# Loading two small factors ahead of the start barrier, with one of them on 32 partitions: a low-rank addition on one core

## Chip, cores, metric

One core of one Trainium2 chip. The metric is device time in microseconds (us), as a median of several executions; before the change it is 123.38 us (three runs, 123.22 to 123.45). A profile is of a single execution; its span leaves out about 1.8 us that the device time includes (121.6 against 123.4 us).

## The reference

```python
# x: (16, 512, 768) float32, A: (768, 16), B: (16, 768), scale = 0.5
lora = np.matmul(np.matmul(x, A), B)
return (x + scale * lora).astype(np.float32)
```

x is 25.2 MB and is read once and written once. A and B are 48 KB each.

## The kernel before

The rows of x are cut into 8 groups of 128 partitions x 8 rows (3 MB, 24,576 contiguous bytes per partition). For each group: ScalarE (ACT) casts x to float16, VectorE (DVE) turns it ("xt"), TensorE (PE) multiplies by A ("y_ps"), ACT writes scaled y into block diagonals ("y_diag"), PE multiplies by B ("lora_ps"), DVE adds in place and the sync queue (SP) stores. Six x buffers are there, so six groups are loaded at once and groups 6 and 7 wait for stores 0 and 1.

```python
def sync_program():
    load(0)                       # then moved into the first block, ahead of the start barrier
    ...
    for g in range(1, X_BUFS):    # X_BUFS = 6
        load(g)
    for g in range(NG - 1):
        nc.sync.wait_ge(added, 4 * (g + 1) + 2)
        nc.sync.dma_start(out=view(out2, g), in_=xs[g % X_BUFS])...
        if g == len(freed) - 1:   # after store 1: loads 6 and 7, each when its buffer is free
            ...
# the last store comes after the block
```

The setup needs A and B. GpSimd (POOL) writes selection matrices and zeros; DVE forms "a16" from A once A has landed and POOL is done; PE spreads it; DVE copies the diagonal blocks to "a_diag". B goes through "b16" and a replicating matmul to "b_rep".

```python
def scalar_program():
    nc.scalar.dma_start(out=a32, in_=A.rearrange("(p m q) r -> p m (q r)", m=NM, q=2)).then_inc(a_in, 16)
    nc.scalar.dma_start(out=b32, in_=B).then_inc(b_in, 16)      # 16 partitions, 3,072 B each
    ...
def vector_program():
    nc.vector.wait_ge(pool_done, 4)
    nc.vector.tensor_tensor(out=a16, ...)._wait_ge(a_in, 16)
    nc.vector.tensor_copy(out=b16[0:R, :], in_=b32)._wait_ge(b_in, 16)
    ...                                                         # a_diag: four copies
    nc.vector.tensor_copy(out=b_rep, in_=b_ps)...
    turn(0, 0, G // 2); turn(0, G // 2, G // 2)
```

Of the kernel before, what the change touches and what calls it, by code (L numbers as in the profile page):

```python
# [1 line left out]

# [7 lines left out]
MM_DT = mybir.dt.float16  # L10
# [4 lines left out]
Q = 32  # L15
# [3 lines left out]
def kernel(  # L19
# [14 lines left out]
    nc = tc.nc  # L34
    fp32 = mybir.dt.float32
    u32 = mybir.dt.uint32
    P = 128
    NQ = P // Q
# [3 lines left out]
    T, D = x2.shape  # L42
    R = A.shape[1]
# [3 lines left out]
    NB = W // Q  # L47
    NM = 4
    PB, PA = Q // NM, W // NM
    assert PA <= P and NM * P <= 512  # L50
    sc = float(scale)

    const = ctx.enter_context(tc.tile_pool(name="const", bufs=1))
    psum = ctx.enter_context(tc.tile_pool(name="psum", bufs=1, space=bass.MemoryType.PSUM))


    x_0 = nc.alloc_sbuf_tensor("x_0", [P, G, D], fp32).ap()
    xs = [x_0] + [const.tile([P, G, D], fp32, name=f"x_{i}") for i in range(1, X_BUFS)]
    xh = [const.tile([P, G, D], MM_DT, name=f"xh_{i}") for i in range(2)]
    xt = const.tile([P, G, W], u32, name="xt")  # L60
    y_diag = const.tile([P, G, P], MM_DT, name="y_diag")


    a32 = const.tile([PA, NM, 2 * R], fp32, name="a32")
    mine = const.tile([PA, NB], MM_DT, name="mine")
    wrap = const.tile([PB, PA], MM_DT, name="wrap")
    step = const.tile([PB, NM, NQ, Q], MM_DT, name="step")
    sel = const.tile([PA, NM, P], MM_DT, name="sel")
    b32 = const.tile([R, D], fp32, name="b32")
    rep = const.tile([Q, NQ * Q], MM_DT, name="rep")  # L70
    a16 = const.tile([PA, NM, NB, 2 * R], MM_DT, name="a16")
    b16 = const.tile([Q, D], MM_DT, name="b16")
    a_diag = const.tile([P, 2 * NB, P], MM_DT, name="a_diag")
    b_rep = const.tile([P, D], MM_DT, name="b_rep")
    y_ps = psum.tile([P, G, Q], fp32, name="y_ps")
    lora_ps = [psum.tile([P, 2, D], fp32, name=f"lora_ps_{i}") for i in range(2)]
# [8 lines left out]
    a_in, b_in = semaphore("a_in"), semaphore("b_in")  # L85
# [17 lines left out]
    def load(g):  # L103
        nc.sync.dma_start(out=xs[g % X_BUFS], in_=view(x2, g)).then_inc(loaded[g], 16)

    def sync_program():
        symbolic, nc._always_lower_symbolic_ap = nc._always_lower_symbolic_ap, False
        load(0)
        nc._always_lower_symbolic_ap = symbolic

        now, first = nc.cur_bb.bb.instructions, nc.main_func.blocks[0].instructions
        at = next(
            k for k, i in enumerate(first)
            if i.engine == mybir.EngineType.SP and isinstance(i, mybir.InstDrain)
        )
        first.insert(at, now.pop())
        for g in range(1, X_BUFS):
            load(g)
        for g in range(NG - 1):
            nc.sync.wait_ge(added, 4 * (g + 1) + 2)  # L120
            nc.sync.dma_start(out=view(out2, g), in_=xs[g % X_BUFS]).then_inc(
                freed[g] if g < len(freed) else stored, 16
            )
            if g == len(freed) - 1:
                for n in range(X_BUFS, NG):
                    nc.sync.wait_ge(freed[n - X_BUFS], 16)
                    load(n)

        nc.sync.wait_ge(added, 4 * NG + 2)
        nc.sync.sem_clear(range(nums[0], nums[-1] + 1))  # L130

    def pool_program():
        nc.gpsimd.sem_clear(stored)

        nc.gpsimd.memset(rep, 0.0)
        nc.gpsimd.memset(wrap, 0.0)
        nc.gpsimd.memset(step, 0.0)
        nc.gpsimd.memset(mine, 1.0).then_inc(pool_done, 1)
        nc.gpsimd.affine_select(
            out=rep.rearrange("i (a k) -> i a k", a=NQ),  # L140
            in_=rep.rearrange("i (a k) -> i a k", a=NQ),
            compare_op=mybir.AluOpType.not_equal, fill=1.0, base=0,
            pattern=[[0, NQ], [-1, Q]], channel_multiplier=1,
        )._wait_ge(pool_done, 1)

        nc.gpsimd.affine_select(
            out=wrap.rearrange("j (b k) -> j b k", k=PB),
            in_=wrap.rearrange("j (b k) -> j b k", k=PB),
            compare_op=mybir.AluOpType.not_equal, fill=1.0, base=0,
            pattern=[[0, NB], [-1, PB]], channel_multiplier=1,  # L150
        )

        nc.gpsimd.affine_select(
            out=step, in_=step,
            compare_op=mybir.AluOpType.not_equal, fill=1.0, base=0,
            pattern=[[1, NM], [0, NQ], [-1, Q]], channel_multiplier=NM,
        )

        nc.gpsimd.affine_select(
            out=mine, in_=mine, compare_op=mybir.AluOpType.is_ge, fill=0.0, base=0,  # L160
            pattern=[[-PB, NB]], channel_multiplier=1,
        ).then_inc(pool_done, 1)
        nc.gpsimd.affine_select(
            out=mine, in_=mine, compare_op=mybir.AluOpType.is_ge, fill=0.0, base=PB - 1,
            pattern=[[PB, NB]], channel_multiplier=-1,
        )._wait_ge(pool_done, 2).then_inc(pool_done, 1)
        nc.gpsimd.memset(b16, 0.0)
        nc.gpsimd.memset(a_diag, 0.0)
        nc.gpsimd.memset(y_diag, 0.0).then_inc(pool_done, 1)

# [4 lines left out]
        return i  # L175

    def scalar_program():
        nc.scalar.dma_start(
            out=a32, in_=A.rearrange("(p m q) r -> p m (q r)", m=NM, q=2)
        ).then_inc(a_in, 16)  # L180
        nc.scalar.dma_start(out=b32, in_=B).then_inc(b_in, 16)

        nc.scalar.copy(out=sel.rearrange("p m k -> p (m k)"), in_=sel_ps)._wait_ge(
            setup_pe, 1
        ).then_inc(setup_act, 1)
        cast(0, 0, G // 2)._wait_ge(loaded[0], 16)
        cast(0, G // 2, G // 2)
        cast(1, 0, G)._wait_ge(loaded[1], 16)
        for g in range(NG):
            for a in range(NQ):  # L190
                q = ds(a * Q, Q)
                i = nc.scalar.mul(out=y_diag[q, :, q], in_=y_ps[q, :, :], mul=sc)  # L192
                if a == 0:
                    i._wait_ge(ready, min(g + 3, NG + 1) + g + 1)
            i.then_inc(spread, 1)
            if g + 2 < NG:
                cast(g + 2, 0, G)._wait_ge(loaded[g + 2], 16)

    a_ps = lora_ps[0][:, 0, 0 : 2 * NB * R]
    b_ps = lora_ps[1][:, 0, :]  # L200
    sel_ps = lora_ps[0].rearrange("p s d -> p (s d)")[0:PA, 512 : 512 + NM * P]

    def turn(g, s0, n):
        rows = ds(s0, n)
        i = nc.vector.transpose(  # L205
            out=xt[:, rows, :].rearrange("p s w -> p (s w)"),
            in_=xh[g % 2][:, rows, :].rearrange("p s d -> p (s d)").bitcast(u32),
        )
        i.then_inc(turned, 1)
        return i  # L210

    def vector_program():
        nc.vector.wait_ge(pool_done, 4)
        nc.vector.tensor_tensor(  # L214
            out=a16,
            in0=a32[:, :, None, :].to_broadcast([PA, NM, NB, 2 * R]),
            in1=mine[:, None, :, None].to_broadcast([PA, NM, NB, 2 * R]),
            op=mybir.AluOpType.mult,
        )._wait_ge(a_in, 16).then_inc(setup_dve, 1)
        nc.vector.tensor_copy(  # L220
            out=b16[0:R, :], in_=b32
        )._wait_ge(b_in, 16).then_inc(setup_dve, 1)
        for a in range(NQ):
            q = ds(a * Q, Q)
            i = nc.vector.tensor_copy(  # L225
                out=a_diag[q, :, ds(a * Q, R)], in_=a_ps[q, :].rearrange("p (b r) -> p b r", r=R)
            )
            if a == 0:
                i._wait_ge(setup_pe, 2)
        nc.vector.tensor_copy(out=b_rep, in_=b_ps)._wait_ge(setup_pe, 3).then_inc(added, 2)  # L230
        turn(0, 0, G // 2)._wait_ge(ready, 1)
        turn(0, G // 2, G // 2)._wait_ge(ready, 2)
        for g in range(NG):
            if g + 1 < NG:
                turn(g + 1, 0, G)._wait_ge(ready, 2 * g + 4)
            for s in range(0, G, 2):
                n = (g * G + s) // 2
                rows = xs[g % X_BUFS][:, ds(s, 2), :]
                nc.vector.tensor_tensor(  # L239
                    out=rows, in0=rows, in1=lora_ps[n % 2], op=mybir.AluOpType.add  # L240
                )._wait_ge(ups, n + 1).then_inc(added, 1)

    def chunks(c0, n):

        while n:
            k = min(n, 512 - c0 % 512)
            yield c0, k
            c0, n = c0 + k, n - k

    def tensor_program():  # L250
# [9 lines left out]
            if m == 0:  # L260
                i._wait_ge(setup_dve, 1)
        i.then_inc(setup_pe, 1)
        for c0, n in chunks(0, D):
            i = nc.tensor.matmul(
                b_ps[:, ds(c0, n)], rep, b16[:, ds(c0, n)], start=True, stop=True
            )
            if c0 == 0:
                i._wait_ge(setup_dve, 2)
        i.then_inc(setup_pe, 1)
        xt_mm = xt.rearrange("p s w -> p (s w)").bitcast(MM_DT)  # L270
# [69 lines left out]
```

## Time and profile before

| what | value | view |
|---|---|---|
| device time | 123.38 us | runs |
| DMA share from 12 to 110 us | 1.00 to 1.01 | table by stretches |
| A issued, landed | 0.96, 11.4 us | timeline, chain |
| first y matmul | 21.37 us | timeline |
| last store issued | 109.83 us | timeline |
| its time to landing | 10.6 us | waits of the SP queue |
| last data packet ends | 120.4 us | packet records of the trace |

The page's DMA strip (40 equal slices, busy share of the 16 DMA engines in tenths) and its queue lines (packets, MB, share of 16 engines' span):

```profile
DMA  7999999999999999999999999999999999999990
...
q1 hardware_dynamic: 2304, 50.33, 97.3%
q10 hardware_dynamic: 144, 0.10, 0.3%
```

q1 is x in and out, q10 is A and B. The table by stretches gives start:end, length, busy time of PE, PEld, DVE, ACT and POOL with counts, the granted PE clock, the DMA share and GB/s:

```profile
0.00:3.00 3.00, 0.00 (x0) 0.00 (x0) 0.00 (x0) 0.80 (x1) 2.05 (x11) 1.00 0.79 229
...
12.00:45.00 33.00, 17.03 (x82) 9.17 (x82) 24.85 (x17) 22.52 (x13) 0.00 (x0) 0.95 1.00 429
45.00:80.00 35.00, 20.87 (x148) 13.42 (x148) 33.95 (x19) 21.21 (x18) 0.00 (x0) 1.00 1.01 431
80.00:110.00 30.00, 14.70 (x96) 8.53 (x96) 26.28 (x14) 9.33 (x12) 0.00 (x0) 0.97 1.00 432
```

No stretch between 12 and 110 us leaves the DMA engines idle, while DVE, the busiest compute engine, is nearly full in only one of them. The timeline (start us, duration us, engine, line, operation, idle time before and its releaser):

```profile
0.96 0.41 ACTq L178 DMA_DIRECT2D a_70<-in_A_dram  x1
...
11.44 1.75 DVE L214 TENSOR_TENSOR a_77<-a_70,mine 96x1536 f16<-96x1536 f32 x1 [11.44 <-DMA a_70<-in_A_dram]
...
21.37 5.20 PE L275 MATMUL y_ps<-xt,a_diag 128*128 128x256 f16 x24 [5.92 <-DVE xt L205]
...
109.83 0.33 SPq L304 DMA_DIRECT2D out_dram<-x_61  x1
```

The waits of the SP queue (who waited, for what: us in total, times, longest) end with the last store:

```profile
SPq L335 <- DMA out_dram<-x_61: 10.6, 1, 10.6
```

And the chain of work that ended last, in order of time (start, us, what), shows the first three y groups of PE:

```profile
21.37 5.21 PE y_ps L275 x24
...
34.81 3.58 PE y_ps L275 x24
...
45.98 2.69 PE y_ps L275 x24
```

After A's landing, with which it begins, this chain is made of compute throughout, because it is followed back from the last instruction that is counted; the store that follows is not in it. The chain has some 98 us of compute work almost without a gap, from 11.4 to 109.3 us.

### The profile page before, as it was taken

How to read it: one execution, taken by the hardware profiler on the slowest of the kernel's cores; microseconds unless marked ns; L12 is line 12 of the kernel's file. 1: busy time of each engine (PE TensorE's matmuls, PEld its weight loads, DVE VectorE, ACT ScalarE, POOL GpSimd, SP SyncE). 2: the span in 40 equal slices, each digit the busy share in tenths (PEclk: the TensorE clock that was granted, in tenths of full speed). 3: DMA queues.
4: the chain of work that ended last, by engine and by line, in shares of the span. 5: the costliest groups of instructions: out<-in, count | busy, mean ns of one | idle time of the engine just before them, and what ended most of it. 6: DMA issues, size and time to landing. Idle time of an engine off the chain costs nothing.

```text
span 121.6 us, 908 instructions
## 1 busy us (share of the span) xinstructions
PE 53.3 (44%) x327; PEld 31.3 (26%) x327; DVE 85.6 (70%) x48; ACT 56.5 (46%) x43; POOL 6.8 (6%) x16
## 2 busy tenths in 40 slices
PE   0200600974296449437446742943754594310000
PEld 0000100642154227216213521821432262100000
DVE  0002699029994999999999999999999982990000
ACT  2305929729903990992596299089440004000000
POOL 6950000000000000000000000000000000000000
PEclk9999999999959999999999999999999999985555
DMA  7999999999999999999999999999999999999990
GB/s 234 407 405 409 437 445 404 445 445 404 445 445 404 445 429 421 396 485 412 396 493 404 404 485 404 412 461 421 429 445 412 437 445 412 437 445 412 445 437 40
DMA packets 2448, 50.43 MB, mean 415 GB/s; under 512 B 288, under 2 KB 384, under 8 KB 400
## 3 DMA queue, kind: packets, MB, share of 16 engines
q1 hardware_dynamic: 2304, 50.33, 97.3%
q10 hardware_dynamic: 144, 0.10, 0.3%
HBM read 25.26 MB, written 25.17 MB: 415 GB/s over the span
## 4 chain that ended last, share of the span: by engine, by line
DVE 51%; PE 28%; DMA 9%; ACT 1%; issue 1%; ACTq 0%; SPq 0%
DVE xt L205 22%; PE y_ps L275 20%; DMA a_70<-in_A_dram 9%; DVE x_61 L239 8%; DVE x L239 5%; PE lora_ps_83 L289 5%; DVE x_63 L239 3%; DVE x_62 L239 3%; DVE x_65 L239 3%; DVE x_64 L239 3%; DVE a_diag L225 2%; DVE a_77 L214 1%; ACT y_diag L192 1%; PE lora_ps_82 L256 1%; DVE b_rep L230 1%
## 5 line engine op out<-in xcount | busy, mean ns | idle before, releaser
L275 PE MATMUL y_ps<-xt,a_diag 128*128 128x256 f16 x192 | 26.0, 296 | 5.9 <-DVE xt L205 5.9
L192 ACT ACTIVATE y_diag<-y_ps 32x256 f16<-32x256 f32 x32 | 12.0, 375 | 34.0 <-PE y_ps L275 33.7
L289 PE MATMUL lora_ps_82<-b_rep,y_diag 128*128 128x512 f16 (+1 forms) x64 | 13.2, 328 | 28.4 <-ACT y_diag L192 13.6
L275 PEld LDWEIGHTS y_ps<-xt,a_diag 128*128 128x128 f16 x192 | 19.9, 104 | 12.2 <-DVE xt L205 6.6
L205 DVE STREAM_TRANSPOSE xt<-xh_67 128x3072 uint32<-128x3072 uint32 x4 | 13.5, 3379 | 6.1 <-PE y_ps L275 6.1
L289 PE MATMUL lora_ps_83<-b_rep,y_diag 128*128 128x512 f16 (+1 forms) x64 | 13.7, 339 | 6.7 <-DVE x_61 L239 1.7
L205 DVE STREAM_TRANSPOSE xt<-xh_66 128x3072 uint32<-128x3072 uint32 (+1 forms) x5 | 13.6, 2728 | 2.3 <-PE y_ps L275 2.3
L289 PEld LDWEIGHTS lora_ps_82<-b_rep,y_diag 128*128 128x128 f16 x64 | 4.9, 97 | 35.8 <-issue 15.9
L173 ACT CAST xh_66<-x 128x3072 f16<-128x3072 f32 (+1 forms) x3 | 10.7, 3604 | 5.5 <-DMA x<-in_x_dram 5.5
L173 ACT CAST xh_67<-x_61 128x6144 f16<-128x6144 f32 x2 | 10.6, 5312 | 2.4 <-DMA x_61<-in_x_dram 2.4
L214 DVE TENSOR_TENSOR a_77<-a_70,mine 96x1536 f16<-96x1536 f32 x1 | 1.8, 1753 | 11.4 <-DMA a_70<-in_A_dram 11.4
L289 PEld LDWEIGHTS lora_ps_83<-b_rep,y_diag 128*128 128x128 f16 x64 | 5.7, 100 | 13.1 <-DVE x_61 L239 2.5
L239 DVE TENSOR_TENSOR x_61<-x_61,lora_ps_82 128x1536 f32<-128x1536 f32 x4 | 7.0, 1740 | 2.8 <-PE lora_ps_82 L289 2.8
L239 DVE TENSOR_TENSOR x_61<-x_61,lora_ps_83 128x1536 f32<-128x1536 f32 x4 | 7.0, 1744 | 0.0
L239 DVE TENSOR_TENSOR x<-x,lora_ps_83 128x1536 f32<-128x1536 f32 x4 | 7.0, 1741 | 0.0
L239 DVE TENSOR_TENSOR x<-x,lora_ps_82 128x1536 f32<-128x1536 f32 x4 | 6.9, 1729 | 0.0
L256 PE MATMUL lora_ps_82<-a_77,sel 96*128 96x384 f16 x4 | 1.5, 521 | 8.9 <-DVE a_77 L214 8.9
L173 ACT CAST xh_66<-x_62 128x6144 f16<-128x6144 f32 x1 | 5.3, 5312 | 0.0
L173 ACT CAST xh_67<-x_63 128x6144 f16<-128x6144 f32 x1 | 5.3, 5312 | 0.0
L173 ACT CAST xh_66<-x_64 128x6144 f16<-128x6144 f32 x1 | 5.3, 5312 | 0.0
L173 ACT CAST xh_67<-x_65 128x6144 f16<-128x6144 f32 x1 | 5.3, 5312 | 0.0
L239 DVE TENSOR_TENSOR x_64<-x_64,lora_ps_83 128x1536 f32<-128x1536 f32 x2 | 3.5, 1742 | 0.0
(33 smaller groups left out, 39.5 us busy)
## 6 DMA issues: line engine op xcount, KB each, us to landing
x<-in_x_dram SPq DMA_DIRECT2D x2, 3072.0 KB, 12.5
x_61<-in_x_dram SPq DMA_DIRECT2D x2, 3072.0 KB, 16.1
out_dram<-x SPq DMA_DIRECT2D x2, 3072.0 KB, 16.0
out_dram<-x_61 SPq DMA_DIRECT2D x2, 3072.0 KB, 12.3
x_62<-in_x_dram SPq DMA_DIRECT2D x1, 3072.0 KB, 24.2
x_63<-in_x_dram SPq DMA_DIRECT2D x1, 3072.0 KB, 30.8
x_64<-in_x_dram SPq DMA_DIRECT2D x1, 3072.0 KB, 37.5
x_65<-in_x_dram SPq DMA_DIRECT2D x1, 3072.0 KB, 44.4
```

The costliest lines, as they stand in the source:

```text
L173: i = nc.scalar.copy(out=xh[g % 2][:, rows, :], in_=xs[g % X_BUFS][:, rows, :])
L192: i = nc.scalar.mul(out=y_diag[q, :, q], in_=y_ps[q, :, :], mul=sc)
L205: i = nc.vector.transpose(out=xt[:, rows, :].rearrange("p s w -> p (s w)"), in_=xh[g % 2][:, rows, :].rearrange("p s d -> p (s d)").bitcas ...
L214: nc.vector.tensor_tensor(out=a16, in0=a32[:, :, None, :].to_broadcast([PA, NM, NB, 2 * R]), in1=mine[:, None, :, None].to_broadcast([PA, ...
L225: i = nc.vector.tensor_copy(out=a_diag[q, :, ds(a * Q, R)], in_=a_ps[q, :].rearrange("p (b r) -> p b r", r=R))
L230: nc.vector.tensor_copy(out=b_rep, in_=b_ps)._wait_ge(setup_pe, 3).then_inc(added, 2)
L239: nc.vector.tensor_tensor(out=rows, in0=rows, in1=lora_ps[n % 2], op=mybir.AluOpType.add)._wait_ge(ups, n + 1).then_inc(added, 1)
L256: i = nc.tensor.matmul(a_ps, sel[:, m, :], a16[:, m].rearrange("p b r -> p (b r)"), start=(m == 0), stop=(m == NM - 1),)
L275: i = nc.tensor.matmul(y_ps, a_diag[:, k, :], xt_mm[:, :, k // 2, :, k % 2], start=(k == 0), stop=(k == 2 * NB - 1),)
L289: i = nc.tensor.matmul(flat[:, ds(c0, w)], y_diag[:, s + k, :], b_rep[:, ds(c0 - k * D, w)], start=True, stop=True,)
```

## The change

The intent: A and B should arrive earlier, by being issued on the scalar queue ahead of the start barrier (as load 0 already was), and B should be spread over partitions 96 to 127, half a row in each, beside A on partitions 0 to 95. The b_rep copy also moves behind the first two turns, and POOL no longer zeroes b16.

```diff
+    ab = nc.alloc_sbuf_tensor("ab", [P, D // H], fp32).ap()          # H = 2
-    a32 = const.tile([PA, NM, 2 * R], fp32, name="a32")
+    a32 = ab[0:PA, 0 : NM * 2 * R].rearrange("p (m r) -> p m r", m=NM)
-    b32 = const.tile([R, D], fp32, name="b32")
+    b32 = ab[HB:, 0 : D // H]                                        # HB = 96
...
-        nc.scalar.dma_start(out=a32, in_=A...).then_inc(a_in, 16)
-        nc.scalar.dma_start(out=b32, in_=B).then_inc(b_in, 16)
+        with ahead(mybir.EngineType.Activation):                     # ahead of the barrier
+            nc.scalar.dma_start(out=a32, in_=A...).then_inc(a_in, 16)
+            nc.scalar.dma_start(
+                out=b32, in_=B.rearrange("r (h c) -> (r h) c", h=H)
+            ).then_inc(b_in, 16)
...
-        nc.gpsimd.memset(b16, 0.0)
...
-        nc.vector.tensor_copy(out=b_rep, in_=b_ps)._wait_ge(setup_pe, 3).then_inc(added, 2)
         turn(0, 0, G // 2)._wait_ge(ready, 1)
         turn(0, G // 2, G // 2)._wait_ge(ready, 2)
+        nc.vector.tensor_copy(
+            out=b_rep.rearrange("p (h c) -> p h c", h=H), in_=b_ps
+        )._wait_ge(setup_pe, 3).then_inc(added, 2)
...
-        for c0, n in chunks(0, D):                                   # 512 and 256 columns
-            i = nc.tensor.matmul(b_ps[:, ds(c0, n)], rep, b16[:, ds(c0, n)], ...)
+        for h in range(H):                                           # twice 384 columns
+            i = nc.tensor.matmul(b_ps[:, h, :], take[HB:, h]..., b16[HB:], ...)
```

## The prediction

> **What bounds the kernel now.** The 16 DMA engines, not the chain of compute. The strip of 40 slices shows DMA at 9 in 38 of 40; the table by stretches shows a DMA share of 0.99 to 1.01 from 3 to 110 us and only 0.79 in 0 to 3 us. Queue q1 (x in and out) takes 97.3% of 16 engines' span. In the trace's packet records every engine moves 128 packets of 24,576 B of 912 ns each, an estimate of 128 x 0.912 = 116.7 us from those numbers. The first starts at 1.0 us and the last ends at 120.4 us, so about 2.7 us is lost on the slowest engine: cold first packets (1.2 to 2.3 us instead of 0.91), A and B, and about 1 us of scattered slow packets. The last store is issued at 109.8 us but needs 10.6 us (waits of the SP queue), while 3 MB need 7.3 us: it stands behind the store before it. So a result that is ready earlier only waits longer.
>
> **What the change does to the front.** Now A is issued at 0.96 us (timeline), its first packet starts at 5.3 us, and A is what the chain waits for until 11.4 us; then a16 1.75, selection matmuls 1.48, a_diag 2.26, b_rep 0.96, turns 3.4, first y matmul at 21.4 us. The diff issues A and B about 1 us earlier[...]. [...] A's six packets per engine come one per x packet, 0.93 us apart. I estimate A landed at 6 to 7.5 us and B at 8 to 9.5. POOL's last memset ends at 7.84 us; without the b16 memset (0.73), with a later barrier, about 7.5. So a16 runs at about 7.5 to 9.3, a_diag is done near 13, and the first turn then waits for x_0's cast (x_0 lands at 10.5, half a cast 2.75 us): turns end near 17.6 us. b_rep's 0.96 us moves under the y matmuls. The first y matmul starts about 3.7 us earlier, near 17.7, and the last store is issued near 106 us.
>
> **How much is on the path that counts.** Nearly nothing of those 3.7 us. The DMA gains are small: B's 3,072-byte packets into 16 partitions coincide with x packets of 1.1 to 1.2 us at 11 us and 0.95 to 1.0 at 12 us, about 0.3 us per engine including B itself. [...]
>
> **Predicted: 123.1 us, 122.5 to 123.7 eight times in ten.** Chances: faster by over 2% 0.02, within 2% 0.97, slower 0.01.
>
> **Right if:** a16 begins before 8.5 us, the first y matmul near 17.7 us, the last store's issue moves to about 106 us and its time to landing grows to about 14 us, while the last packet still ends at 119.8 to 120.6 us; DMA share stays 1.0 from 12 to 110 us; no slow x packets at 11 to 12 us.
>
> **Wrong if:** the last packet moves with the last store's issue (then compute bounded the end); the DMA share drops below 1 in the middle; the two issues ahead of the barrier delay load 0's first packet by over 0.5 us; or earlier stores slow the 912 ns packets.

The forecast came to 123.1 us, 0.3 us below the 123.38 us of before. Two terms stood behind that: 0.2 us for B's new layout, an estimate out of the 0.3 us per engine that the records have beside B, and 0.1 us that A and B might win, or lose again, at the start.

## The result and the profile after

The time did not move: 123.30 us (four runs, 123.20 to 123.43) against 123.37 (four runs). The ratio is 0.9996 with a 95% interval of 0.9979 to 1.0014. Ratios are the mean time of one kernel's fast runs over that of the other's in the same rounds, so they are not quite the ratio of the quoted medians. A second measurement over five rounds (after_again below) gave 0.9992, 0.9973 to 1.0012.

The same lines of the page after:

```profile
DMA  7999999999999999999999999999999999999991
...
q1 hardware_dynamic: 2304, 50.33, 97.6%
q10 hardware_dynamic: 160, 0.10, 0.3%
```

The table by stretches after:

```profile
0.00:3.00 3.00, 0.00 (x0) 0.00 (x0) 0.00 (x0) 1.28 (x1) 1.38 (x9) 1.00 0.79 221
...
12.00:45.00 33.00, 18.99 (x88) 10.00 (x89) 25.41 (x18) 22.99 (x13) 0.00 (x0) 0.91 1.01 430
45.00:80.00 35.00, 20.43 (x144) 13.10 (x142) 32.92 (x18) 21.50 (x18) 0.00 (x0) 0.99 1.01 429
80.00:110.00 30.00, 14.70 (x96) 8.54 (x96) 25.68 (x14) 8.74 (x11) 0.00 (x0) 1.00 1.00 432
```

The timeline after:

```profile
0.13 0.39 ACTq L190 DMA_DIRECT2D ab<-in_A_dram  x1
...
10.46 1.75 DVE L229 TENSOR_TENSOR a<-ab,mine 96x1536 f16<-96x1536 f32 x1 [10.46 <-DMA ab<-in_A_dram]
...
19.53 5.30 PE L293 MATMUL y_ps<-xt,a_diag 128*128 128x256 f16 x24 [5.05 <-DVE xt L220]
...
109.23 0.34 SPq L322 DMA_DIRECT2D out_dram<-x  x1
```

The waits of the SP queue after:

```profile
SPq L353 <- DMA out_dram<-x: 11.0, 1, 11.0
```

The chain after:

```profile
19.53 5.32 PE y_ps L293 x24
...
32.70 4.06 PE y_ps L293 x24
...
44.98 3.08 PE y_ps L293 x24
```

Three things are to be read here. First, the DMA engines are as full as before and the last packet ends at 120.1 instead of 120.4 us. Second, A is issued 0.83 us earlier and lands 0.98 us earlier (10.46 against 11.44), no more than that, so that the first y matmul comes 1.84 us earlier: 0.98 from A and 0.96 from b_rep, which now runs under the y matmuls, less small change. Third, of those 1.84 us only 0.60 are left when the last store is issued (109.23 against 109.83), and even those 0.60 us turn into a longer time to landing (11.0 against 10.6 us).

### The profile page after: what moved, and what is told of

The parts are those of the page before. It is cut to its first block, busy times and chain, and to the rows that moved or that the text cites. A ratio compares the mean times of both kernels' runs of the same rounds, so it can differ in the third digit from the quotient of the medians.

```text
span 121.3 us, 907 instructions
## 1 busy us (share of the span) xinstructions
PE 54.8 (45%) x327; PEld 31.8 (26%) x327; DVE 85.5 (71%) x48; ACT 56.4 (47%) x43; POOL 6.5 (5%) x15
## 4 chain that ended last, share of the span: by engine, by line
DVE 49%; PE 29%; DMA 8%; issue 2%; ACT 1%
DVE x L256 25%; PE y_ps L293 21%; DVE xt L220 21%; DMA ab<-in_A_dram 8%; PE lora_ps L307 6%; DVE a_diag L240 2%; DVE a L229 1%; ACT y_diag L206 1%; PE lora_ps L273 1%
## 5 line engine op out<-in xcount | busy, mean ns | idle before, releaser
L256 DVE TENSOR_TENSOR x<-x,lora_ps 128x1536 f32<-128x1536 f32 x32 | 53.7, 1737 | 2.8 <-PE lora_ps L307 2.8
L184 ACT CAST xh<-x 128x6144 f16<-128x6144 f32 (+1 forms) x9 | 42.6, 4743 | 6.7 <-DMA x<-in_x_dram 6.5
L307 PE MATMUL lora_ps<-b_rep,y_diag 128*128 128x512 f16 (+1 forms) x128 | 26.1, 339 | 34.8 <-DVE x L256 21.2
L220 DVE STREAM_TRANSPOSE xt<-xh 128x3072 uint32<-128x3072 uint32 (+1 forms) x9 | 27.1, 3018 | 8.7 <-PE y_ps L293 8.6
L293 PE MATMUL y_ps<-xt,a_diag 128*128 128x256 f16 x192 | 27.0, 303 | 5.1 <-DVE xt L220 5.1
L307 PEld LDWEIGHTS lora_ps<-b_rep,y_diag 128*128 128x128 f16 x128 | 10.7, 99 | 49.1 <-DVE x L256 27.7
L293 PEld LDWEIGHTS y_ps<-xt,a_diag 128*128 128x128 f16 x192 | 20.4, 107 | 12.0 <-DVE xt L220 5.7
L229 DVE TENSOR_TENSOR a<-ab,mine 96x1536 f16<-96x1536 f32 x1 | 1.8, 1755 | 10.5 <-DMA ab<-in_A_dram 10.5
L273 PE MATMUL lora_ps<-a,sel 96*128 96x384 f16 x4 | 1.5, 521 | 6.8 <-DVE a L229 6.8
L240 DVE CAST a_diag<-lora_ps 32x384 f16<-32x384 f32 x4 | 2.2, 554 | 0.9 <-PE lora_ps L273 0.9
L179 POOL MEMSET a_diag<- 128x3072 f16 x1 | 2.7, 2653 | 0.0
```

Of the source, the lines that this page charges most:

```text
L179: nc.gpsimd.memset(a_diag, 0.0)
L184: i = nc.scalar.copy(out=xh[g % 2][:, rows, :], in_=xs[g % X_BUFS][:, rows, :])
L220: i = nc.vector.transpose(out=xt[:, rows, :].rearrange("p s w -> p (s w)"), in_=xh[g % 2][:, rows, :].rearrange("p s d -> p (s d)").bitcas ...
L229: nc.vector.tensor_tensor(out=a16, in0=a32[:, :, None, :].to_broadcast([PA, NM, NB, 2 * R]), in1=mine[:, None, :, None].to_broadcast([PA, ...
L240: i = nc.vector.tensor_copy(out=a_diag[q, :, ds(a * Q, R)], in_=a_ps[q, :].rearrange("p (b r) -> p b r", r=R))
L256: nc.vector.tensor_tensor(out=rows, in0=rows, in1=lora_ps[n % 2], op=mybir.AluOpType.add)._wait_ge(ups, n + 1).then_inc(added, 1)
```

## Experiments

The question is not why the time changed, but whether it is really the DMA engines that hold it, how close compute is behind them, why A came so late all the same, and where the compute gain went. The theory: the 16 DMA engines bound the kernel, and a store that is issued earlier only stands longer in line. The main rival: the compute chain bounds it, and the change's gain was eaten by something new.

All runs in one table. "Issued" is the last store's issue, "landing" its time to landing, both from the profile of that run; "last packet" is the end of the last 24,576-byte packet in the packet records. The ratio is against the kernel before in the same rounds.

| run | median us | ratio, 95% interval | issued | landing | last packet |
|---|---|---|---|---|---|
| before | 123.38 | | 109.83 | 10.6 | 120.4 |
| the change | 123.30 | 0.9996 (0.9979 to 1.0014) | 109.23 | 11.0 | 120.1 |
| after_again | 123.19 | 0.9992 (0.9973 to 1.0012) | 107.50 | 12.7 | 120.1 |
| ahead_only | 123.32 | 1.0017 (0.9986 to 1.0049) | 106.85 | 13.1 | 119.9 |
| layout_only | 123.97 | 1.0058 (1.0004 to 1.0112) | 109.27 | 11.7 | 120.9 |
| mid | 123.29 | 0.9993 (0.9977 to 1.0010) | 105.68 | 14.6 | 120.1 |
| a_first | 124.45 | 1.0084 (1.0059 to 1.0108) | 107.00 | 14.9 | 121.9 |
| warm | 123.40 | 1.0016 (0.9991 to 1.0041) | 107.90 | 12.4 | 120.2 |
| warm_full | 123.36 | 0.9985 (0.9958 to 1.0012) | 106.93 | 14.3 | 121.2 |
| first_warm | 124.06 | 1.0096 (1.0021 to 1.0171) | 105.51 | 15.6 | 120.9 |
| thin_add (wrong result) | 123.49 | 1.0016 (0.9998 to 1.0034) | 98.00 | 23.5 | 121.5 |
| late_1 | 123.45 | 1.0005 (0.9985 to 1.0024) | 107.82 | 13.0 | 120.8 |
| late_2 | 124.49 | 1.0043 (1.0003 to 1.0083) | 113.51 | 8.3 | 121.8 |
| late_3 | 129.52 | none (three of four runs slow) | 118.20 | 8.4 | 126.5 |

### Compute made far shorter: thin_add

The changed kernel, with additions over 32 of 768 columns. Its output is wrong, which doesn't matter for the time.

```diff
-    out=rows, in0=rows, in1=lora_ps[n % 2], op=mybir.AluOpType.add
+    out=rows[:, :, 0:32], in0=rows[:, :, 0:32],
+    in1=lora_ps[n % 2][:, :, 0:32], op=mybir.AluOpType.add,
```

> Wrong result on purpose: the additions treat 32 of 768 columns, so that DVE loses about 1.6 of 1.74 us in each of 32 additions, some 50 us in all. Theory (the 16 DMA engines bound the kernel): stores are issued many us earlier, and the total stays within 1% of 123.3 us. Rival (the compute chain that ends with the last addition bounds it): the total falls by over 10 us.

The table by stretches of thin_add, and below it the waits of its SP queue:

```profile
45.00:80.00 35.00, 17.29 (x117) 11.06 (x115) 12.04 (x14) 19.10 (x16) 0.00 (x0) 0.84 1.01 428
80.00:110.00 30.00, 13.43 (x88) 8.45 (x86) 5.38 (x11) 6.52 (x9) 0.00 (x0) 0.78 1.00 432
```

```profile
SPq L354 <- DMA out_dram<-x: 23.5, 1, 23.5
```

DVE's busy time fell from 85.6 to 38.1 us, its 33 us in the stretch from 45 to 80 us became 12, and the last store was issued 11 us earlier. It then took 23.5 us to land, and the time was the same within 0.2%. This settles the main question: shorter compute is worth nothing here.

### Compute made later: late_1, late_2, late_3

POOL gets extra memsets ahead of the semaphore that releases DVE's first product. They write buffers that are not used yet ("xt", and a spare one), so there is no race.

```diff
+        xt_h = xt.rearrange("p s w -> p (s w)").bitcast(MM_DT)
+        nc.gpsimd.memset(xt_h[:, 0:4096], 0.0)        # late_1, late_2, late_3
+        nc.gpsimd.memset(spare, 0.0)                  # late_2, late_3: 5,120 elements
+        nc.gpsimd.memset(spare, 0.0)                  # late_3, behind a semaphore of the first
         nc.gpsimd.memset(y_diag, 0.0).then_inc(pool_done, 1)
```

> The changed kernel with one more memset of 4096 elements on POOL ahead of the semaphore that releases DVE's first product: an estimate of 3.5 us from a_diag's memset (3072 elements, 2.65 us), so a16 starts near 11.8 instead of 10.5 us. Theory (DMA bound, with slack of about 1.5 to 2 us between the last store's issue at 109.2 us and the moment at which the engines reach it): the last store's issue moves to about 110.5 us, total within 0.3%. Rival (compute bound): total up by about 1.3 us.

> As late_1 with a second memset of 5120 elements (an estimate of 4.4 us): a16 near 16.2 us, 5.7 us later than in the changed kernel. Theory: the last store is issued near 115 us, some 3 us after the engines ran dry, so the DMA share falls below 1 at about 112 us and the total grows by 2.5 to 4.5 us, that is, by the delay less the slack. Rival of full compute bound: up by 5.7 us. Rival that the store's issue never matters: no growth.

> As late_2 with the second memset done twice (4.15 us more by the POOL records of late_2): a16 starts near 20.3 us, 9.8 us later than in the changed kernel. Theory: the last store is issued at 116.5 to 119.5 us; the engines run dry at about 111.5 us, and the total grows to 128 to 132 us. The growth over late_2 is close to 1 us for each us of later issue, and the runs spread by more than 1 us, as the half-clock stretches now count. Rival (late_2's growth was a one-off of the DMA): total under 126 us.

The table by stretches of late_2 shows the engines run dry just before its last store:

```profile
110.00:112.00 2.00, 0.55 (x4) 0.15 (x2) 2.00 (x2) 0.00 (x0) 0.00 (x0) 0.97 1.08 467
112.00:114.00 2.00, 0.00 (x0) 0.00 (x0) 1.00 (x1) 0.00 (x0) 0.00 (x0) 0.50 0.21 86
114.00:116.00 2.00, 0.00 (x0) 0.00 (x0) 0.00 (x0) 0.00 (x0) 0.00 (x0) 0.50 0.93 393
```

The DMA share drops to 0.21 in 112 to 114 us. The waits of the SP queue, of late_2 and then of late_3:

```profile
SPq L357 <- DMA out_dram<-x: 8.3, 1, 8.3
```

```profile
SPq L359 <- DMA out_dram<-x: 8.4, 1, 8.4
```

A store that finds the engines idle needs 8.3 us to land, twice alike. That gives the slack: in the kernel before the last store landed at 109.83 + 10.6 = 120.4 us, so it could have been issued as late as 120.4 - 8.3 = 112.1 us, 2.3 us later than it was, at no cost. late_2 issued it 1.4 us beyond that point and lost 0.43% (0.5 us) in its fast runs, with 1.7 us in the profiled one (last packet at 121.8 instead of 120.1). late_3 issued it at 118.20 us and its last packet ended 8.3 us later. Between the profiles of late_2 and late_3 the issue moved by 4.69 us and the last packet by 4.70 us: once the slack is used up, compute counts one to one in this pair of profiles. A caution: late_3's profile is of a run that was put down as slow, because three of its four runs (129.5 to 129.7 us) were over 1.5% above the fastest (126.81). That delay costs time is shown by the fast run of 126.81 us too, which is above every fast run of the kernel before.

late_3 also ran dry in the middle (DMA share 0.73 from 45 to 60 us), as store 0 came late as well.

Three sizes were missed. late_1 was to issue its last store near 110.5 us; although its first y matmul was 1.33 us later than in the changed kernel (20.86 against 19.53), its last store was 1.41 us earlier. late_2 was to lose 2.5 to 4.5 us and lost less, as its store came at 113.5 and not at 115 us. late_3 was to take 128 to 132 us; its three slow runs did, and its fast run took 126.81. In late_1 and late_2 the half clock of PE, below, accounts for it (the granted clock from 12 to 45 us is 0.95 in both, 0.91 in the changed kernel): against the changed kernel their chains spend 2.75 and 1.35 us less in the first three y groups and the lora_ps pieces between them. late_3's fast run has no profile, so its cause is not shown.

### One half of the change at a time: ahead_only, layout_only

ahead_only is the kernel before with A and B issued ahead of the barrier, B still on 16 partitions. layout_only is the changed kernel with both issued after the barrier.

```diff
 # ahead_only, against the kernel before
+        with ahead(mybir.EngineType.Activation):
             nc.scalar.dma_start(out=a32, ...); nc.scalar.dma_start(out=b32, in_=B)...
 # layout_only, against the changed kernel
-        with ahead(mybir.EngineType.Activation):
             nc.scalar.dma_start(out=a32, ...); nc.scalar.dma_start(out=b32, in_=B.rearrange(...))...
```

> The kernel before, with A and B only issued ahead of the barrier, and B still on 16 partitions. Theory (the slow x packets near 11 us come from B's 3,072-byte packets going to 16 partitions): A's first packet near 3.5 us and A landed near 10.4 us, as in the changed kernel, but the x packets beside B still take 1.1 to 1.2 us. Rival (those slow packets come from the place in time): none over 1.05 us. Both: total within 0.3% of the kernel before.

> The changed kernel with A and B issued after the barrier, as before. Theory: A's first packet near 5.3 us and A landed near 11.4 us, so a16 starts at 11.4; no x packet over 1.05 us beside B, so the layout alone removes the slow packets. First y matmul at 20.4 us (1 us of the move is b_rep after the turns). Rival: slow packets of 1.1 to 1.2 us stay. Both: total within 0.3%.

From the packet records, not a view of the profile: the x packets that start between 9.3 and 13.5 us, while B passes (912 ns is the undisturbed time of one).

```
              over 1,050 ns   longest ns   time over 912 ns, sum / 16 engines
before              16           1224            0.31 us
ahead_only          13           1226            0.26 us
layout_only          0            981            0.07 us
the change           0           1000            0.09 us
```

So with B on the scalar queue its layout, and not the moment of its issue, removes the slow packets, and it is worth about 0.2 us per engine. It is not the whole cause: mid, below, has the same layout, but A and B packed into 9.0 to 10.1 us behind load 0 in the sync queue, and there 14 x packets of this window took over 1,050 ns again (longest 1,120, 0.20 us per engine). The layout has B on 32 partitions instead of 16, and in packets half as large (1,536 instead of 3,072 B); no run tells the two apart. The gain is not seen in the time. The end is set by the slowest engine: in the kernel before, 14 of the 16 engines wrote their last completion record between 118.9 and 119.6 us, the other two at 120.1 and 120.4. That spread is larger than the 0.2 us.

The start times came as expected: a16 at 10.7 us or so in ahead_only (the chain has A landed at 0.13 + 10.56 us), at 11.63 in layout_only. layout_only's first y matmul, expected at 20.4 us, came at 20.82. layout_only was slower by 0.58%, where 0.3% was the limit of what I expected. Its profiled run has one engine that ended at 120.9 us; why, I can't say.

### Where A is in the queues: a_first, mid

```diff
 # a_first: on the sync queue ahead of load 0; mid: behind load 0
         with ahead(mybir.EngineType.SP):
+            nc.sync.dma_start(out=a32, in_=A...).then_inc(a_in, 16)      # a_first
+            nc.sync.dma_start(out=b32, in_=B...).then_inc(b_in, 16)      # a_first
             load(0)
+            nc.sync.dma_start(out=a32, in_=A...).then_inc(a_in, 16)      # mid
+            nc.sync.dma_start(out=b32, in_=B...).then_inc(b_in, 16)      # mid
-        with ahead(mybir.EngineType.Activation): ...
```

> The changed kernel with A and B issued on the sync queue ahead of load 0, so that their packets stand in front of x in the same rings. Theory (A is late because each of its six packets per engine waits for one 0.93 us x packet, and because its ring is reached only after 2.5 us): A lands before 4 us, a16 is then released by POOL near 8.3 us, the first y matmul starts near 17.7 us as the prediction had it. Rival (A is late for a fixed cost of small transfers at the start): A still lands after 8 us. Total: both expect within 0.5%; if load 0 is pushed back by the two issues (about 0.8 us of sequencer time) the total may grow by up to 0.8 us, as the DMA engines bound it.

> The changed kernel with A and B on the sync queue behind load 0 and ahead of load 1. Theory for the run with A first (it lost 1 us because load 0's first packets started 0.5 us and more later, behind two issues and their packets): here load 0's first packet is at 1.0 us again, A lands near 9.8 us just behind load 0, and the total is within 0.4% of the kernel before. Rival (it lost because A and B share x's rings): total up by about 0.8% again.

("Rings", in these two expectations, means the packets of a queue in the order in which they are moved.)

In the changed kernel the packet records have A's first 512-byte packet at 3.5 us, although it was issued at 0.13 us and load 0's first packet started at 1.0 us; A's last one ends at 9.0 us. The six packets per engine came about 0.93 us apart, one after each x packet. Ahead of its first packet of A, each engine had taken two of load 0's (32 packets over 16 engines, by count), the first of them a cold one of 1.5 to 2.2 us; in the kernel before, where A was issued 0.83 us later, it was about four (63 packets). Why two and not one stays open. In a_first all of A's packets lie between 1.02 and 1.43 us. So A is late because of its place behind x, not because a small transfer takes long. The timeline of a_first:

```profile
0.00 0.39 SPq L129 DMA_DIRECT2D ab<-in_A_dram  x1
0.45 0.41 SPq L132 DMA_DIRECT2D ab<-in_B_dram  x1
0.90 3.72 SPq L109 DMA_DIRECT2D x<-in_x_dram  x6
...
8.65 1.75 DVE L227 TENSOR_TENSOR a<-ab,mine 96x1536 f16<-96x1536 f32 x1 [8.65 <-POOL y_diag L186]
...
11.36 5.41 ACT L190 CAST xh<-x 128x3072 f16<-128x3072 f32 x2 [4.98 <-DMA x<-in_x_dram]
...
16.80 1.78 DVE L218 STREAM_TRANSPOSE xt<-xh 128x1536 uint32<-128x1536 uint32 x1 [0.79 <-ACT xh L190]
...
18.64 1.67 PE L291 MATMUL y_ps<-xt,a_diag 128*128 128x256 f16 x7 [5.97 <-DVE xt L218]
```

a16 is now released by POOL, as the prediction had it for the change itself, and the second turn, and with it the first y matmul, waits for x_0's cast (11.36 to 16.77 us; the 0.79 us ahead of the turn end with it). It comes at 18.64 us: the predicted 17.7 plus the 0.9 us by which x_0 landed later than predicted (11.36 instead of 10.5).

But a_first is 0.84% slower, about 1 us, where I had allowed 0.5%, or 0.8 us at most: the DMA engines are the bound, and it pushes load 0 back. Load 0 is issued at 0.90 us, behind A and B, and in the packet records its first packet starts at 1.95 instead of 1.01 us, 0.94 us later. (The expectation for mid speaks of 0.5 us; that is where B's first packet starts, at 1.49 us.) This agrees with the median's loss. The profile is of the slowest of the four runs (124.87 us), and its last packet ends 1.8 us later than in the changed kernel. The rest of that shows in its records near 45 us, where loads give way to stores: the time over 912 ns of the packets that start between 43 and 48 us sums to 15.9 us over 16 engines, 1.0 us each, with single packets of 2.5 us, against 3.9 us, 0.24 us each, in the changed kernel (0.94 and 0.76 make 1.7). Why this switch is dearer there stays open; in the other runs whose engines were busy at the switch it varied between 1.7 and 9.8 us in sum. mid, which has A and B in the same queue but behind load 0, has its first x packet at 1.0 us and is as fast as the others, so sharing the queue is not the cost. A landed at 10.6 us there, not at 9.8: its packets ended at 9.9.

### The clock of PE: warm, warm_full, first_warm, after_again

The gain of 1.84 us at the first y matmul fell to 0.60 us at the last store. The two chains say where: the first three y groups took 5.32 + 4.06 + 3.08 = 12.46 us after and 5.21 + 3.58 + 2.69 = 11.48 us before, which is 0.98 us. The two pieces of lora_ps between them in the chain (1.09 + 1.46 us after, 1.46 + 0.82 before) took 0.27 us more. Together 1.25 us, and 1.84 - 1.25 = 0.59.

The table by stretches of y_ps's instructions alone, of the kernel before and then of the changed one:

```profile
32.00:40.00 8.00, 3.78 (x24) 2.83 (x24) 1.50 (x4) 0.79 1.02 439
40.00:50.00 10.00, 2.84 (x24) 2.29 (x24) 1.28 (x4) 1.00 0.99 420
```

```profile
32.00:40.00 8.00, 4.25 (x24) 3.04 (x24) 1.50 (x4) 0.79 1.01 433
40.00:50.00 10.00, 3.28 (x24) 2.58 (x24) 1.50 (x4) 0.83 1.01 425
```

The clock (the third number from the end) is below 1 in one stretch before and in two after. In the trace's clock records these are stretches of 3.41 us at 0.5 each: at 33.15 us before, at 32.03 and 42.27 us after. In them the y matmuls start 213 ns apart; at 1.0 they start 111 ns apart. The first y group lies almost wholly ahead of the first clock record, which begins, at 1.0, at 26.33 us before and at 25.20 us after; there the view shows 1.00 (12 to 32 us) although the matmuls start 213 ns apart, as in the stretches at 0.5. I take the first group for half clock by that spacing. What sets such a stretch off is not shown, and their number differs from run to run: the same kernel, run again as after_again, had one such stretch and not two (0.95 from 12 to 45 us instead of 0.91), and issued its last store at 107.50 instead of 109.23 us.

> The changed kernel once more, for a narrower interval and a second profile. Theory: total 0 to 0.3% below the kernel before, if the 0.2 us of slow packets saved beside B count at all, else the same; last store's issue anywhere from 106.5 to 109.5 us, by how many half-clock stretches fall on its first y groups, with the last packet at 119.8 to 121 us whatever it is.

In after_again the total and the last packet (120.1 us) are the same as in the first profile although the last store was issued 1.73 us earlier. The change's own two profiles thus differ by more than the change moved the store.

Is the first y group faster if PE works ahead of it? Both runs add 22 spare matmuls between setup and the first y group, whose result is overwritten.

```diff
+        for k in range(22):
+            nc.tensor.matmul(y_ps[0:96]..., wrap, step[...])                        # warm: 8 rows, 96 columns
+            nc.tensor.matmul(y_ps..., y_diag[:, k % 8, :], xh[0][...])              # warm_full: 128 rows, 128 columns
```

> The changed kernel with 22 spare matmuls (their result is overwritten) between the setup matmuls and the first y group, to keep PE busy from about 14.5 to 19 us. Theory (the front's gain of 1.8 us shrank to 0.6 us at the last store because PE ran its first three y groups at the half clock: 5.3, 4.1 and 3.1 us instead of 2.7): the first y group takes 2.7 to 3.5 us, the last store's issue moves to about 106 to 107.5 us. Total within 0.3%, as DMA bounds it. Rival (the first y group is slow for another reason, such as cold buffers): it still takes 5.3 us.

> As the run with spare matmuls, but each spare matmul now uses all 128 rows and columns of the array (y_diag, still zero, against x) in place of 8 rows and 96 columns. Theory [...]: the half clock is released before 19 us and the first y group takes 2.7 to 3.5 us; the last store is issued near 106 to 108 us; total within 0.3%. Rival [...]: the first y group still takes over 4.2 us.

The PE timeline of warm, then of warm_full:

```profile
14.14 4.47 PE L290 MATMUL y_ps<-step,wrap 8*96 8x256 f16 x20
19.55 5.14 PE L299 MATMUL y_ps<-xt,a_diag 128*128 128x256 f16 x24 [0.94 <-DVE xt L221]
```

```profile
14.71 3.72 PE L291 MATMUL y_ps<-xh,y_diag 128*128 128x256 f16 x22
19.83 2.85 PE L302 MATMUL y_ps<-xt,a_diag 128*128 128x256 f16 x24 [1.40 <-DVE xt L221]
```

My expectation for warm failed: 22 small matmuls right ahead of the first y group left it at 5.14 us, and the first clock record begins at 24.4 us, 4.9 us after the first y matmul (in the kernel before and the changed one it is 5.0 and 5.7 us). With the full-size ones, which had zero weights, it begins at 17.1 us, 2.4 us after the first of them, and the first y group took 2.85 us. So the slow first group is the half clock, and 22 small matmuls, from 13.7 to 18.6 us, did not end it. warm_full was profiled once. What counts in the larger ones is not told apart: they used more rows and columns, and they moved x itself instead of a selection matrix, which is mostly zeros. In warm_full a half-clock stretch at 30.8 us then made the second y group slow (4.05 us), and the last store was issued at 106.93 us. In warm it was 107.90, where 106 to 107.5 was expected. The time did not follow in either run.

> A and B first on the sync queue, and the spare matmuls as well: the earliest compute of all. Theory: last store issued before 106.5 us, its time to landing grows to 13 us or more, total within 0.5% of the kernel before. Rival (compute bound): total falls by as much as the issue moves, 3 us or more.

first_warm puts A first and adds the small spare matmuls. It issued its last store at 105.51 us, 4.3 us before the kernel before, and was slower (1.0096, where 0.5% was expected at most), with the same late load 0 as a_first: its first x packet starts at 1.97 us. It is the clearest case of a trade against the bound: 4 us of compute bought with about one microsecond of DMA, and the result a loss.

No version was found that beats both kernels. The packet records say why none was near: 2,048 packets of 24,576 B over 16 engines are 128 each, an estimate of 128 x 0.912 = 116.7 us from the records' own 912 ns, of the 119.4 us between the first packet and the last one's end. In the kernel before, the sixteen first packets take 0.74 us longer than 0.912 us on average, the packets beside B 0.31 us per engine, the switch near 45 us 0.11, and the slowest engine ends about 1.2 us after the middle one; that leaves about 0.3 us.

## Why the prediction was right, and where its steps were not

- **The bound: right.** It named the DMA engines, and said that a result that is ready earlier only waits longer. thin_add shows it (11 us earlier, 23.5 us to land, same time), and late_2 and late_3 show the other side: past 112 us a later issue of the last store delays the end, one to one between their two profiles (late_3's is of a slow run). The predicted 123.1 us (122.5 to 123.7) holds the measured 123.30.
- **The DMA gain of 0.2 us: right in size where it arises, not seen in the time.** No x packet near 11 us is over 1.05 us any more; 0.31 us per engine became 0.09. The spread between engines at the end, over 1 us, and the intervals of the ratios, some 0.2 us to each side, are too wide to show it; that it reaches the end at all is not shown.
- **A landed at 6 to 7.5 us: wrong.** It landed at 10.46. The prediction reckoned that A's packets would start beside load 0's, which no trace had shown. Its first packet came 2.5 us after load 0's (3.5 against 1.0 us), behind two x packets per engine, and then each further one waited for an x packet, about 0.93 us. Only putting A on the sync queue ahead of load 0 came near the predicted front (a16 at 8.65 us instead of 7.5).
- **First y matmul near 17.7 us, 3.7 us earlier: wrong by half.** It came at 19.53, 1.84 us earlier, half of which is b_rep's copy moved away.
- **Last store at about 106 us with about 14 us to landing: wrong.** 109.23 and 11.0 us in the first profile, 107.50 and 12.7 in the second. Besides the smaller gain at the front, the step lacked the half-clock stretches of PE, which differ from run to run: the two profiles' last stores lie 1.73 us apart, more than the 0.60 us that were gained.
- **The last packet between 119.8 and 120.6 us, the DMA share 1.0 from 12 to 110 us: right** (120.1; 1.01, 1.01, 1.00).

The outcome was forecast for the right reason, and that is not luck; the size of the compute gain was wrong by half, and as none of it counts, this did no harm. It would have in a kernel where the slack of 2.3 us was not there.

## What to carry to other kernels

Before shortening a compute chain, look at how long the last store takes to land against what a store into idle engines takes: the difference (here 10.6 - 8.3 = 2.3 us) says that the transfers are the bound, and how far compute is behind it. A chain of waits made almost wholly of compute is no proof, since it may leave out the transfer at its end. A small transfer issued on a second queue beside a stream of large packets landed here by its place among them (A was issued at 0.13 us, its packets ran from 3.5 to 9.0 us), and moving it ahead of the stream was paid for with the stream (A's packets from 1.02 to 1.43 us, load 0's first packet 0.94 us later, the kernel 0.84% slower).
